# Gating rows' scale and shift applied after the spatial product, and the sample states updated one per two units across the output projection and the u units

## The chip, the cores and the metric

The kernel runs on one core of one Trainium2 chip. The metric is the device time of one execution in microseconds; the profile is of one such execution on the same core. TensorE is called PE, VectorE DVE, ScalarE ACT, GpSimd POOL, and SP is the engine that issues most of the DMAs.

## The reference

The kernel is one inference step of a two-layer hybrid decoder trunk on a prompt of 512 tokens and on 8 sample tokens, all in f32 with a width of 1024. Layer 0 mixes with retention and a chunked gating unit, layer 1 with a convolution module, and each is followed by a squared-ReLU MLP. The part that the change touches is the mixer of layer 0:

```python
z = h @ w_in
q, k, v, g, u, s = jnp.split(z, SPLIT_IDX, axis=-1)
...
o, s_new = retention(q, k, v, s0.astype(jnp.float32))   # S_n = gamma S_{n-1} + k_n^T v_n
...
u = jax.nn.gelu(u, approximate=False)
s = jax.nn.gelu(s, approximate=False).reshape(b, t, SGU_GROUPS, SGU_GD)
s_n = layernorm32(s.astype(jnp.float32), ln_g.reshape(SGU_GROUPS, SGU_GD),
                  ln_b.reshape(SGU_GROUPS, SGU_GD)).astype(h.dtype)
...
mixed = jnp.einsum('gij,bnjgd->bnigd', w_s, s_n.reshape(b, nc, c, SGU_GROUPS, SGU_GD)) \
    + bias[:, :, None]
sgu_out = u * mixed.reshape(b, t, U_W)
y = jnp.concatenate([ret_out, sgu_out], axis=-1) @ w_out
return y, s_new, s_n.reshape(b, t, U_W)
```

`w_s` is a causal 128x128 matrix per group, `ln_g` and `ln_b` are per feature. The new retention states of the 8 samples (8 x 4 heads x 128 x 256) and the normalized rows `s_n` of the 8 sample tokens are outputs.

## The kernel before

**Units.** Activations lie feature by token, as 8 chunks of 128 features by 520 tokens. A projection is done in units: one unit makes 128 output features from a 128x1024 block of weights (512 KB, `load_w`, L122, one DMA on SP into one of four `raw` buffers). To keep f32 precision the weights are split in two halves of four chunks each, into a rounded high part on ACT (L132) and the rest on DVE (L133), `wh` and `wl`, with five buffers for half units. PE then does three products per chunk and half of the tokens (`unit_mm`, L161; `unit_part`, L178, for one half of the tokens): 48 matmuls of 260 columns per unit into a two-bank PSUM tile. There are two such tiles (`mmt`, L103), so a unit starts when the unit before the last has been read out of PSUM by DVE.

**The stages around the change.** After the g and v units come eight s units (`in_units(4096, C)`, L722). Each is read out of PSUM by DVE (L724), put through gelu on ACT and, once per group of two units, handled by `s_tok` (L686): PE transposes the tokens to rows (L697), ACT copies them out, DVE takes mean and variance (L707, L708), does an inverse root in small steps (`rsqrt`, L300) and normalizes in place (L714), and POOL multiplies by the scale rows (L716) and adds the shift rows (L717), 128x1024 per group, and the same for the 8 sample rows (L719, L720). The scale and shift rows are loaded as `ln_row`, broadcast to 128 partitions (L683). In the same stage the retention of the last head is finished (`ret_last`, `ret_gate`) and the samples' retention runs: `ret_sample` (L630) loads each of the 8 states on POOL's queue and multiplies it into `os`, and `ret_sample_out` (L649) normalizes the result and writes the sample columns of `reth` and `retl` (L665, L667).

Then come eight units of the retention half of the output projection, `opr` (L745), of which the first two are done half by half; DVE adds each to `x` (L753), which takes the buffer of a tile that is read last in `ret_sample_out`. Then come the eight u units (L762): DVE reads the unit (L765), ACT does gelu (L766), PE multiplies the normalized rows by the spatial matrix (`mx`, L769), DVE adds the position bias (L772) and multiplies by gelu(u) (L775), and the product is split for the next projection (`sguh` on ACT, L399, and `sgul` on DVE, L400). Last the other half of the output projection, `ops` (L801), with the state sums of the convolution's history (`hist`, L787, L791) beside the end of the u units.

**The sample states' update.** `ret_update(b)` (L635) is written at the end of each u unit. It loads state b again (512 KB, on POOL's queue, into one of three `s0` buffers), loads the sample's v row broadcast to 128 partitions in two parts `vb` (256 KB each, on SP, two `kx` buffers), scales them by k on ACT (L644, four steps), forms gamma x S + k v on DVE (L645, four steps) and stores the state on POOL's queue (L647).

**What sets the order.** Each engine runs its own queue in order. The order is made at build time by a scheduler that takes instructions by priority (as written) when their buffers and inputs would be ready, so work that is written later can move ahead of work that is written earlier. Hand-made exceptions are `tc.high_priority` (used at L736) and `tc.issue_after(ins)`, which queues what a block traces on the engine of `ins` behind `ins`; instructions of the block on other engines stay free. In the kernel before, the scheduler moved five of the eight updates ahead of the first opr unit's add.

Of the kernel before, what the change touches and what calls it, by code (L numbers as in the profile page):

```python
# [76 lines left out]
def trunk_kernel(tc, a, o):  # L77
    nc = tc.nc
    te, ve, se, pe_ = nc.tensor, nc.vector, nc.scalar, nc.gpsimd
    with ExitStack() as st:  # L80
# [34 lines left out]
        def h2(ap):  # L115
            return ap.rearrange("p (h t) -> p h t", h=2)
# [149 lines left out]
        def const(name, shape, ap=None, eng=None):  # L266
            t = cp.tile(shape, F32, name=name)
            if ap is not None:
                (eng or nc.sync).dma_start(t, ap)
            return t  # L270
# [2 lines left out]
            return cp.tile([P, C, TS], F32, name=name, tag="small", bufs=2)  # L273

        x0 = bigt("x0")
        par = const("par", [P, 15, C], a["par"], nc.scalar)
        (G_MIX0, G_FFN0, G_MIX1, G_FFN1, G_FIN, GN_G, B_A, B_G, DW_B, CLN_G, CLN_B, B_OUT, W00, SB0, _S) = range(15)

        def pcol(i, c):
            return par[:, i, c:c + 1]  # L280
# [116 lines left out]

        def split_act(src, hi, lo):
            se.activation(hi, src, AF.Copy)  # L399
            ve.tensor_sub(lo, src, hi.bitcast(F32))  # L400
# [224 lines left out]
        def ret_state(b):  # L625
            S0 = mp.tile([P, NH, DV], F32, name="S0", tag="s0", bufs=3)
            nc.gpsimd.dma_start(S0, a["state_ret"][b].rearrange("h d e -> d h e"))
            return S0

# [2 lines left out]
            for h in range(NH):  # L632
                te.matmul(os_[32 * h:32 * h + TS, :], qm[:, h, b, :], S0[:, h, :], start=False, stop=b == TS - 1)

        def ret_update(b):  # L635
            S0 = ret_state(b)
            vb = []
            for i in range(2):
                t = mp.tile([P, 2 * DV], F32, name="vb", tag="kx", bufs=2)
                nc.sync.dma_start(t, scr[b:b + 1, i * 2 * DV:(i + 1) * 2 * DV].to_broadcast([P, 2 * DV]))  # L640
                vb.append(t)
            for h in range(NH):
                vh = vb[h // 2][:, (h % 2) * DV:(h % 2 + 1) * DV]
                se.activation(vh, vh, AF.Copy, scale=ks[:, h, b:b + 1])  # L644
                ve.scalar_tensor_tensor(out=S0[:, h, :], in0=S0[:, h, :], scalar=float(GAMMA[h]), in1=vh,  # L645
                                        op0=ALU.mult, op1=ALU.add)
# [32 lines left out]
        ln_t = {}  # L679
        for hf in range(2):  # L680
            for i in range(2):
                t = mp.tile([P, 544], F32, name="ln_row", tag="qk", bufs=8)[:, :512]
                nc.sync.dma_start(t, a["sgu_ln"][i:i + 1, hf * 512:(hf + 1) * 512].to_broadcast([P, 512]))  # L683
                ln_t[i, hf] = t

        def s_tok(g):  # L686
            sn = mp.tile([P, NC, DV], F32, name=f"sn{g}", tag="vtm", bufs=NH)
            s_n.append(sn)
            sd = ss_n[:, g * DV:(g + 1) * DV]
            for i in range(3):  # L690
                at_ = aux(f"st{g}_{i}")
                rows = P if i < 2 else TS
                subs = 2 if i < 2 else 1
                for u in range(subs):
                    tok = slice((2 * i + u) * P, (2 * i + u) * P + rows)
                    for j in range(2):
                        te.transpose(at_[:rows, u * DV + j * P:u * DV + (j + 1) * P], gs[2 * g + j][:, tok], ident)  # L697
# [18 lines left out]
            pe_.tensor_tensor(sn, sn, gg.rearrange("p (o e) -> p o e", o=1).to_broadcast([P, NC, DV]), op=ALU.mult)  # L716
            pe_.tensor_tensor(sn, sn, bb.rearrange("p (o e) -> p o e", o=1).to_broadcast([P, NC, DV]), op=ALU.add)  # L717
            dst = ss_n[:, g * DV:(g + 1) * DV]
            pe_.tensor_mul(dst, dst, gg[:TS])  # L719
            pe_.tensor_add(dst, dst, bb[:TS])  # L720

        for c, pt in in_units(4096, C):  # L722
            t = tmp(f"s{c}")
# [18 lines left out]
        x = bigt("x")  # L742
        for c in range(C):
            nc.sync.dma_start(x[:, c, :], a["xT"][:, c, :])
        for c in range(C):  # L745
            pt = mmt(f"opr{c}")
            w = split_w(load_w(a["ab_w_out"], 0, c * P))
            if c < 2:
                for hf in range(2):
                    unit_part(pt[:, hf, :HALF], w, two(reth, retl), slice(hf * HALF, (hf + 1) * HALF))  # L750
            else:
                unit_mm(halves(pt), w, two(reth, retl))
            ve.tensor_tensor(h2(x[:, c, :]), ph2(pt), h2(x[:, c, :]), op=ALU.add)  # L753


        ssT = small("ssT")
# [2 lines left out]
            te.transpose(at_[:, c * TS:(c + 1) * TS], ss_n[:, c * P:(c + 1) * P], ident[:TS, :TS])  # L759
        se.copy(ssT, at_[:, :C * TS].rearrange("p (c t) -> p c t", c=C))  # L760
        sguh, sgul = bigt("sguh", F32R), bigt("sgul", F32R)
        for c, pt in in_units(3072, C):  # L762
            g = c // 2
            t = tmp(f"u{c}")
            ve.tensor_tensor(h2(t), ph2(pt), h2(r0), op=ALU.mult)  # L765
            se.activation(t, t, AF.Gelu)  # L766
            at_ = aux(f"mx{c}")
            for n in range(NC):
                te.matmul(at_[:, n * P:(n + 1) * P], s_n[g][:, n, (c % 2) * P:(c % 2 + 1) * P], wsT[:, g, :],  # L769
                          start=True, stop=True)  # L770
# [4 lines left out]
            ve.tensor_mul(m, m, t)  # L775
# [412 lines left out]
```

## Time and profile before

| what | value |
|---|---|
| median of 3 runs | 1317.03 us (1313.05 to 1317.89) |
| the profiled execution | 1319.12 us, of it the span of the trace 1317.4 us |
| mean granted PE clock | 0.985 |
| busy PE, DVE, ACT, POOL | 1273.5, 923.0, 648.7, 242.7 us |
| DMA | 149.21 MB, mean 113 GB/s |

A window of the trace gives each engine's busy time in a stretch of the span, the clock that PE was granted (1.00 is full speed), and the share of the 16 DMA engines. A timeline row gives start, duration, engine, line, operation, output and inputs, and in square brackets how long the engine had been idle and what released it. A line can be that of a helper: L133 is every split of weights, whatever its stage.

### The profile page before, as it was taken

The page shows a single profiled execution, that of the slowest core. Times are in us where ns is not written, and L with a number is a line of the kernel's source. Part 1 is how long each engine was busy: PE and PEld are TensorE (multiplying, and loading weights), DVE is VectorE, ACT ScalarE, POOL GpSimd, SP SyncE. Part 2 cuts the span into 40 slices and gives each one's busy share as a digit, 9 for nine tenths or more (in the row PEclk, how much of TensorE's full clock was granted, in tenths as well). Part 3 has the DMA queues.
Part 4 walks back from the last instruction along what each step waited for, and adds up shares of the span by engine and source line. Part 5 has one row for each costly group of instructions (what it writes and reads, how often), then busy time and mean ns, then how long its engine had stood idle before and what let it go on. Part 6 is the DMA issues. An engine that isn't in the chain of part 4 may idle for free.

```text
span 1317.4 us, 26073 instructions
## 1 busy us (share of the span) xinstructions
PE 1273.5 (97%) x10618; PEld 1241.4 (94%) x10618; DVE 923.0 (70%) x1634; ACT 648.7 (49%) x1160; POOL 242.7 (18%) x226
## 2 busy tenths in 40 slices
PE   9999999799999999999999999989989999999996
PEld 8999999799998999999999998858989999999995
DVE  6833668965688866766755699968997667676544
ACT  7432343433356643544444476547756445454342
POOL 0521013640020000000000469842200000000012
PEclk9999999899999999999999999999989999999998
DMA  7323235773222323332322322453523333332321
GB/s 281 97 86 104 85 130 193 249 278 111 81 82 81 99 94 97 97 113 81 114 96 96 93 85 81 140 129 112 161 65 97 103 90 101 109 97 81 97 81 65
DMA packets 50407, 149.21 MB, mean 113 GB/s; under 512 B 6112, under 2 KB 13280, under 8 KB 50288
## 3 DMA queue, kind: packets, MB, share of 16 engines
q1 hardware_dynamic: 45888, 134.11, 33.1%
q0 software_dynamic: 3456, 12.58, 2.7%
q8 instruction: 83, 1.36, 0.4%
q10 hardware_dynamic: 944, 0.86, 0.2%
q14 instruction: 36, 0.29, 0.1%
HBM read 139.35 MB, written 9.13 MB: 113 GB/s over the span
## 4 chain that ended last, share of the span: by engine, by line
PE 85%; DVE 9%; issue 2%; ACT 2%; DMA 1%; DVEq 0%; SPq 0%
PE y L161 27%; PE in L161 15%; PE pp L245 12%; PE pq L245 6%; PE ci L161 4%; PE ops L161 3%; PE pr L245 3%; PE f L161 3%; PE opr L161 3%; DVE wl L133 2%; PE co L178 2%; DVE cv L1023 2%; PE cvB L993 1%; PE opr L178 1%; ACT wh L132 0%
## 5 line engine op out<-in xcount | busy, mean ns | idle before, releaser
L132 ACT ACTIVATE wh<-raw 128x512 fp32r<-128x512 f32 x403 | 252.3, 629 | 347.2 <-PE in L161 101.9
L133 DVE TENSOR_TENSOR wl<-raw,wh 128x512 fp32r<-128x512 f32 x403 | 301.0, 749 | 165.8 <-ACT wh L132 159.0
L161 PE MATMUL y<-f,wh 128*128 128x260 f32 x2016 | 323.9, 283 | 0.8 <-DVE x L872 0.8
L161 PEld LDWEIGHTS y<-f,wh 128*128 128x128 f32 x2016 | 275.8, 188 | 1.2 <-DVE x L872 1.2
L161 PE MATMUL y<-f,wl 128*128 128x260 f32 x1008 | 202.6, 282 | 0.0
L161 PEld LDWEIGHTS y<-f,wl 128*128 128x128 f32 x1008 | 155.3, 188 | 0.0
L161 PE MATMUL in<-n0h,wh 128*128 128x260 f32 x640 | 133.0, 287 | 1.2 <-DVE k L470 0.8
L161 PE MATMUL in<-n0l,wh 128*128 128x260 f32 x640 | 130.8, 285 | 1.2 <-DVE n0l L358 1.0
L161 PE MATMUL in<-n0h,wl 128*128 128x260 f32 x640 | 129.6, 284 | 0.1
L132 ACT ACTIVATE wh<-S 128x512 fp32r<-128x512 f32 x116 | 73.1, 631 | 91.4 <-PE y L161 45.5
L133 DVE TENSOR_TENSOR wl<-S,wh 128x512 fp32r<-128x512 f32 x116 | 79.3, 687 | 49.6 <-ACT wh L132 48.4
L161 PEld LDWEIGHTS in<-n0h,wh 128*128 128x128 f32 x640 | 99.0, 188 | 3.6 <-PE in L161 1.3
L161 PEld LDWEIGHTS in<-n0l,wh 128*128 128x128 f32 x640 | 98.7, 188 | 2.7 <-DVE n0l L358 2.5
L245 PE MATMUL pp<-Th,wh 128*128 128x260 f32 x348 | 98.3, 283 | 0.9 <-ACT Th L213 0.9
L161 PEld LDWEIGHTS in<-n0h,wl 128*128 128x128 f32 x640 | 98.6, 188 | 0.4 <-DVE wl L133 0.3
L245 PE MATMUL pp<-Tl,wh 128*128 128x260 f32 x348 | 98.1, 282 | 0.0
L245 PE MATMUL pp<-Th,wl 128*128 128x260 f32 x348 | 97.8, 282 | 0.0
L1016 POOL TENSOR_TENSOR pacc<-pacc,pp 128x512 f32<-128x512 f32 x60 | 88.1, 1478 | 4.5 <-ACT pp L1015 1.7
L374 POOL TENSOR_TENSOR n2acc<-n2acc,n2sq 128x520 f32<-128x520 f32 x5 | 7.0, 1402 | 344.9 <-DVE n2l L358 327.3
L374 POOL TENSOR_TENSOR n4acc<-n4acc,n4sq 128x520 f32<-128x520 f32 x5 | 6.5, 1307 | 346.7 <-ACT n4sq L371 346.7
L245 PEld LDWEIGHTS pp<-Th,wh 128*128 128x128 f32 x348 | 65.5, 189 | 1.4 <-ACT Th L213 1.1
L245 PEld LDWEIGHTS pp<-Tl,wh 128*128 128x128 f32 x348 | 65.5, 188 | 0.0
(406 smaller groups left out, 2919.2 us busy)
## 6 DMA issues: line engine op xcount, KB each, us to landing
raw<-in_ffn_w SPq DMA_DIRECT2D x128, 512.0 KB, 3.6
raw<-in_ab_w_in SPq DMA_DIRECT2D x39, 512.0 KB, 3.7
S<-in_state_ret POOLq DMA_DIRECT2D x16, 512.0 KB, 4.8
raw<-in_ab_w_out SPq DMA_DIRECT2D x16, 512.0 KB, 3.7
raw<-in_conv_w_in SPq DMA_DIRECT2D x16, 512.0 KB, 3.7
raw<-in_conv_w_out SPq DMA_DIRECT2D x16, 512.0 KB, 3.7
X<-xscr SPq DMA_DIRECT2D x32, 132.0 KB, 3.3
x<-in_xT SPq DMA_DIRECT2D x16, 260.0 KB, 5.3
```

Source lines behind the costliest of these rows:

```text
L132: se.activation(hi, sp, AF.Copy)
L133: ve.tensor_sub(lo, sp, hi.bitcast(F32))
L161: te.matmul(pts[hf], wt[:, k % KH, :], x(k, SECOND if hf else FIRST)[i == 1], start=k == order[0] and i == 0, stop=k == order[-1] and i == 2)
L178: te.matmul(pt, wt[:, k % KH, :], xt, start=n == 0 and i == 0, stop=n == C - 1 and i == 2)
L245: te.matmul(bank, wt[:, k, :], xt, start=n in (1, 2, 5) and k == 0 and i == 0, stop=k == KH - 1 and i == 2, skip_group_check=True)
L374: eng.tensor_add(self.acc, self.acc, sq)
L993: te.matmul(acc[32 * g:32 * g + 32, :], diag[c, k][:, g, :], X[:, g, k:k + HC], start=k == 0, stop=k == ns - 1)
L1016: pe_.tensor_add(pacc, pacc, pp)
L1023: ve.scalar_tensor_tensor(out=o, in0=win(k), scalar=dw[:, c, k:k + 1], in1=acc, op0=ALU.mult, op1=ALU.add)
```

## The change

1. The scale and shift of the normalized prompt rows are no longer applied before the spatial product. Since the product runs over positions and scale and shift go by feature, `mixed = scale x (W s) + shift x rowsum(W) + bias`. PE makes the row sums of the masked spatial matrix once, for all groups (`wsum`, a product of 128x512 with a matrix of ones), ACT scales them into `ws`, DVE makes `bias_c = ws x shift + bias` per u unit (128x128), and the mixing sum becomes one step with the scale as a column factor. The two columns come in `par` (16 instead of 15). The 8 sample rows keep scale and shift on POOL, and `ln_row` is loaded for 8 partitions.
2. `ret_update` is cut in two, `ret_load` and `ret_update`. `ret_behind(n, done)` is called after each of the eight opr adds (n = 0 to 7) and after each of the eight u units' splits (n = 8 to 15): an even n loads state n // 2, an odd n updates the state loaded before. Its block is queued behind the add or the split on DVE, which binds the four DVE steps of the update; loads, scalings on ACT and stores are free.
3. The first two opr units are written with their first token halves ahead of their second ones.

```diff
-            se.activation(hi, src, AF.Copy)
-            ve.tensor_sub(lo, src, hi.bitcast(F32))
+            return ve.tensor_sub(lo, src, hi.bitcast(F32))
...
-        def ret_update(b):
-            S0 = ret_state(b)
-            vb = []
+        def ret_load(b):
+            S0, vb = ret_state(b), []
...
+            return b, S0, vb
+
+        def ret_update(b, S0, vb):
...
+        loaded = []
+
+        def ret_behind(n, done):
+
+            with tc.issue_after(done.ins):
+                if n % 2:
+                    ret_update(*loaded.pop())
+                else:
+                    loaded.append(ret_load(n // 2))
...
-            pe_.tensor_tensor(sn, sn, gg.rearrange("p (o e) -> p o e", o=1).to_broadcast([P, NC, DV]), op=ALU.mult)
-            pe_.tensor_tensor(sn, sn, bb.rearrange("p (o e) -> p o e", o=1).to_broadcast([P, NC, DV]), op=ALU.add)
...
+        def opr_add(c, pt):
+            ret_behind(c, ve.tensor_tensor(h2(x[:, c, :]), ph2(pt), h2(x[:, c, :]), op=ALU.add))
+
+        first = [(mmt(f"opr{c}"), split_w(load_w(a["ab_w_out"], 0, c * P))) for c in range(2)]
+        for hf, cols in enumerate((FIRST, SECOND)):
+            for c, (pt, w) in enumerate(first):
+                unit_part(pt[:, hf, :HALF], w, ret, cols)
+                if hf:
+                    opr_add(c, pt)
...
+        at_ = aux("wsum")
+        te.matmul(at_, ones, wsT.rearrange("p g i -> p (g i)"), start=True, stop=True)
+        ws = mp.tile([P, 544], F32, name="ws", tag="qk", bufs=8)[:, :TP].rearrange("p (g i) -> p g i", g=NH)
+        se.activation(ws.rearrange("p g i -> p (g i)"), at_, AF.Copy, scale=float(D))
...
+            ve.scalar_tensor_tensor(out=bias_c, in0=ws[:, g, :], scalar=pcol(SLN_B, c), in1=bias_row[:, g, :],
+                                    op0=ALU.mult, op1=ALU.add)
...
-            ve.tensor_tensor(m[:, :TP].rearrange("p (n t) -> p n t", n=NC), at_.rearrange("p (n t) -> p n t", n=NC),
-                             bias_row[:, g:g + 1, :].to_broadcast([P, NC, P]), op=ALU.add)
+            ve.scalar_tensor_tensor(out=m[:, :TP].rearrange("p (n t) -> p n t", n=NC),
+                                    in0=at_.rearrange("p (n t) -> p n t", n=NC), scalar=pcol(SLN_G, c),
+                                    in1=bias_c.rearrange("p (o t) -> p o t", o=1).to_broadcast([P, NC, P]),
+                                    op0=ALU.mult, op1=ALU.add)
...
-            ret_update(c)
+            ret_behind(C + c, done)
```

**How the order moves.** The first place is DVE's queue at the end of the s units, before the change; `s_2919` is the read of the last s unit (`in_7`) out of PSUM, `olny` and `slny` are the inverse roots of the samples' retention and of the gating rows, and `S_3730` is a sample state.

```order
L133 TENSOR_TENSOR wl<-raw,wh 128x512
L656 TENSOR_SCALAR olnv<-omv 128x1
L645 SCALAR_TENSOR_TENSOR S_3730<-S_3730,vb 128x256 x2
L708 BN_AGGR smv<-sst_2792 8x2
L645 SCALAR_TENSOR_TENSOR S_3730<-S_3730,vb 128x256
L304 TENSOR_SCALAR rs_t<-olnv 128x1
L306 TENSOR_SCALAR rs_vh<-olnv 128x1
L645 SCALAR_TENSOR_TENSOR S_3730<-S_3730,vb 128x256
L711 TENSOR_SCALAR slnv<-smv 128x5
L724 TENSOR_TENSOR s_2919<-in_7_2860,n0r 128x520
```

The same place of the changed kernel, where the read is `s_2913`:

```order
L309 TENSOR_TENSOR rs_t<-rs_t,rs_vh 128x1
L309 TENSOR_TENSOR rs_t<-rs_t,rs_vh 128x5
L310 SCALAR_TENSOR_TENSOR olny<-rs_t,olny 128x1
L310 SCALAR_TENSOR_TENSOR slny<-rs_t,slny 128x5
L734 TENSOR_TENSOR s_2913<-in_7_2854,n0r 128x520
L671 TENSOR_SCALAR ons<-os,omv,olny 128x256
```

No state step stands ahead of the read any more, and the two inverse roots, which stood behind it, now stand ahead of it.

The second place is DVE's queue in the u units. Before, around the second u unit:

```order
L765 TENSOR_TENSOR u_3628<-in_1_3569,n0r 128x520
L772 TENSOR_TENSOR m_3636<-mx_3631,bias_row 128x512
L774 TENSOR_SCALAR m_3636<-ssT,par 128x8
L133 TENSOR_TENSOR wl<-raw,wh 128x512
L775 TENSOR_TENSOR m_3636<-m_3636,u_3628 128x520
L133 TENSOR_TENSOR wl<-raw,wh 128x512
L400 TENSOR_TENSOR sgul<-m_3636,sguh 128x520
L765 TENSOR_TENSOR u_3716<-in_2_3657,n0r 128x520
```

And now:

```order
L788 TENSOR_TENSOR u_3677<-in_1_3618,n0r 128x520
L799 TENSOR_SCALAR m_3687<-ssT,par 128x8
L133 TENSOR_TENSOR wl<-raw,wh 128x512
L795 SCALAR_TENSOR_TENSOR m_3687<-mx_3682,par,bias_c 128x512
L800 TENSOR_TENSOR m_3687<-m_3687,u_3677 128x520
L786 SCALAR_TENSOR_TENSOR bias_c<-ws,par,bias_row 128x128
L400 TENSOR_TENSOR sgul<-m_3687,sguh 128x520
L647 SCALAR_TENSOR_TENSOR S_3612<-S_3612,vb 128x256 x4
L133 TENSOR_TENSOR wl<-raw,wh 128x512
L788 TENSOR_TENSOR u_3761<-in_2_3702,n0r 128x520
```

Four state steps stand between the second unit's `sgul` and the read of the third unit, and one split of weights stands behind them.

The third place is ACT's queue there. Before:

```order
L399 ACTIVATE sguh<-m_3636 128x520
L132 ACTIVATE wh<-raw 128x512
L766 ACTIVATE u_3716<-u_3716 128x520
L132 ACTIVATE wh<-raw 128x512
L399 ACTIVATE sguh<-m_3724 128x520
```

And now:

```order
L399 ACTIVATE sguh<-m_3687 128x520
L132 ACTIVATE wh<-raw 128x512 x2
L646 ACTIVATE vb<-vb,ks 128x256
L789 ACTIVATE u_3761<-u_3761 128x520
L646 ACTIVATE vb<-vb,ks 128x256 x3
L399 ACTIVATE sguh<-m_3771 128x520
```

The first scaling of the next update's v row stands ahead of the third unit's gelu, and the other three ahead of its `sguh`.

More of the change, by code (lines that the diff above doesn't have):

```diff
@@ L275, in trunk_kernel @@
         x0 = bigt("x0")
-        par = const("par", [P, 15, C], a["par"], nc.scalar)
-        (G_MIX0, G_FFN0, G_MIX1, G_FFN1, G_FIN, GN_G, B_A, B_G, DW_B, CLN_G, CLN_B, B_OUT, W00, SB0, _S) = range(15)
+        par = const("par", [P, 16, C], a["par"], nc.scalar)
+        (G_MIX0, G_FFN0, G_MIX1, G_FFN1, G_FIN, GN_G, B_A, B_G, DW_B, CLN_G, CLN_B, B_OUT, W00, SB0, SLN_G, SLN_B) = range(16)
         def pcol(i, c):
@@ L681, in trunk_kernel @@
             for i in range(2):
-                t = mp.tile([P, 544], F32, name="ln_row", tag="qk", bufs=8)[:, :512]
-                nc.sync.dma_start(t, a["sgu_ln"][i:i + 1, hf * 512:(hf + 1) * 512].to_broadcast([P, 512]))
+                t = mp.tile([P, 544], F32, name="ln_row", tag="qk", bufs=8)[:TS, :512]
+                nc.sync.dma_start(t, a["sgu_ln"][i:i + 1, hf * 512:(hf + 1) * 512].to_broadcast([TS, 512]))
                 ln_t[i, hf] = t
@@ L715, in s_tok @@
             gg, bb = [ln_t[i, g // 2][:, (g % 2) * DV:(g % 2 + 1) * DV] for i in range(2)]
-            pe_.tensor_tensor(sn, sn, gg.rearrange("p (o e) -> p o e", o=1).to_broadcast([P, NC, DV]), op=ALU.mult)
-            pe_.tensor_tensor(sn, sn, bb.rearrange("p (o e) -> p o e", o=1).to_broadcast([P, NC, DV]), op=ALU.add)
             dst = ss_n[:, g * DV:(g + 1) * DV]
-            pe_.tensor_mul(dst, dst, gg[:TS])
-            pe_.tensor_add(dst, dst, bb[:TS])
+            pe_.tensor_mul(dst, dst, gg)
+            pe_.tensor_add(dst, dst, bb)
         for c, pt in in_units(4096, C):
@@ L744, in trunk_kernel @@
             nc.sync.dma_start(x[:, c, :], a["xT"][:, c, :])
-        for c in range(C):
-            pt = mmt(f"opr{c}")
[L747 to L753, printed above, removed]
+        ret = two(reth, retl)
+        def opr_add(c, pt):
[6 more added lines that the diff above has]
+                    opr_add(c, pt)
+        for c in range(2, C):
+            pt = mmt(f"opr{c}")
+            unit(pt, a["ab_w_out"], 0, c * P, ret)
+            opr_add(c, pt)
         ssT = small("ssT")
@@ L764, in trunk_kernel @@
             t = tmp(f"u{c}")
+            bias_c = mp.tile([P, TP], F32, name="bias_c", tag="on", bufs=4)[:, :P]
+            ve.scalar_tensor_tensor(out=bias_c, in0=ws[:, g, :], scalar=pcol(SLN_B, c), in1=bias_row[:, g, :],
+                                    op0=ALU.mult, op1=ALU.add)
             ve.tensor_tensor(h2(t), ph2(pt), h2(r0), op=ALU.mult)
@@ L771, in trunk_kernel @@
             m = tmp(f"m{c}")
-            ve.tensor_tensor(m[:, :TP].rearrange("p (n t) -> p n t", n=NC), at_.rearrange("p (n t) -> p n t", n=NC),
-                             bias_row[:, g:g + 1, :].to_broadcast([P, NC, P]), op=ALU.add)
+            ve.scalar_tensor_tensor(out=m[:, :TP].rearrange("p (n t) -> p n t", n=NC),
+                                    in0=at_.rearrange("p (n t) -> p n t", n=NC), scalar=pcol(SLN_G, c),
+                                    in1=bias_c.rearrange("p (o t) -> p o t", o=1).to_broadcast([P, NC, P]),
+                                    op0=ALU.mult, op1=ALU.add)
             ve.tensor_scalar(m[:, TP:], ssT[:, c, :], pcol(W00, c), pcol(SB0, c), op0=ALU.mult, op1=ALU.add)
             ve.tensor_mul(m, m, t)
-            split_act(m, sguh[:, c, :], sgul[:, c, :])
-            ret_update(c)
+            done = split_act(m, sguh[:, c, :], sgul[:, c, :])
+            ret_behind(C + c, done)
         dw = const("dw", [P, C, W], a["dw"])
@@ L1144 @@
         feat(np.repeat(g["sgu_w"][0, :, 0, 0], 256)), feat(np.repeat(g["sgu_b"][0, :, 0], 256)),
-        feat(g["final_norm_g"])], 1)
+        feat(g["sgu_ln_g"][0]), feat(g["sgu_ln_b"][0])], 1)
     taps = np.concatenate([g["conv_dw_w"][0], np.zeros((1, D), np.float32)]).reshape(W + 1, C, 4, 32)
```

## The prediction

> **What bounds the kernel now.** I read the page first, then the stretch that the diff touches in windows, then who waited there, then the timelines of the engines that are waited for.
>
> ```profile
> span 1317.4 us, 26073 instructions
> PE 1273.5 (97%) x10618; PEld 1241.4 (94%) x10618; DVE 923.0 (70%) x1634; ACT 648.7 (49%) x1160; POOL 242.7 (18%) x226
> ```
>
> TensorE (PE) carries the time, so a change elsewhere pays only where PE waits or runs slowly. The windows by stage give seconds of busy time for PE, PEld, DVE, ACT and POOL, then the granted clock, the DMA share and GB/s. They are cut at the ends of the s units, of the output projection's retention half (opr) and of the u units.
>
> ```profile
> 182.00:238.00 56.00, 55.80 (x483) 50.62 (x482) 41.81 (x121) 24.26 (x47) 17.44 (x16) 1.00 0.54 183
> 238.00:267.50 29.50, 21.47 (x139) 20.73 (x138) 26.75 (x85) 10.11 (x23) 21.05 (x26) 0.77 0.81 261
> 267.50:302.50 35.00, 35.00 (x294) 34.84 (x292) 21.67 (x40) 13.05 (x25) 10.54 (x8) 1.00 0.70 248
> 302.50:353.20 50.70, 50.70 (x427) 50.70 (x427) 31.20 (x55) 19.02 (x33) 2.89 (x8) 1.00 0.32 98
> ```
>
> PE is full before 238 and after 267.5. Between them it is idle for 29.50 - 21.47 = 8.03 us and its clock falls to 0.77, while DVE is busy for 26.75 of 29.50. That is the only hole in this part. The waits and PE's timeline (start, duration, engine, what, idle time before it) say where it opens:
>
> ```profile
> PE opr L178 <- DVE olny L305: 5.3, 1, 5.3
> PE opr L178 <- DVE retl L400: 2.3, 1, 2.3
> ...
> 240.99 0.28 PE L178 MATMUL opr<-reth,wl 128*128 128x260 f32 x1
> 246.62 0.59 PE L178 MATMUL opr<-reth,wh 128*128 128x260 f32 x1 [5.34 <-DVE olny L305]
> 247.00 0.42 PE L178 MATMUL opr<-retl,wh 128*128 128x260 f32 x1
> 247.22 0.42 PE L178 MATMUL opr<-reth,wl 128*128 128x260 f32 x1
> 259.21 0.58 PE L178 MATMUL opr<-retl,wh 128*128 128x260 f32 x1 [2.31 <-DVE retl L400]
> ```
>
> After the gap a matmul starts every 0.22 us (247.00 to 247.22); at full clock it is 34.60/288 = 0.120 (a row below). Both gaps end on DVE, so I read DVE beside POOL:
>
> ```profile
> 240.91 2.37 POOL L717 TENSOR_TENSOR sn<-sn,ln_row 128x1024 f32<-128x1024 f32 x1
> 252.66 2.37 POOL L716 TENSOR_TENSOR sn<-sn,ln_row 128x1024 f32<-128x1024 f32 x1
> ...
> 232.44 0.69 DVE L133 TENSOR_TENSOR wl<-raw,wh 128x512 fp32r<-128x512 f32 x1 [3.55 <-PE st L697]
> 236.27 0.68 DVE L724 TENSOR_TENSOR s<-in,n0r 128x520 f32<-128x520 f32 x1
> 236.88 2.27 DVE L133 TENSOR_TENSOR wl<-raw,wh 128x512 fp32r<-128x512 f32 x1
> 241.39 2.44 DVE L133 TENSOR_TENSOR wl<-raw,wh 128x512 fp32r<-128x512 f32 x1
> 245.88 0.68 DVE L724 TENSOR_TENSOR s<-in,n0r 128x520 f32<-128x520 f32 x1
> 253.15 2.17 DVE L645 SCALAR_TENSOR_TENSOR S<-S,vb 128x256 f32<-128x256 f32 x1
> 256.51 2.65 DVE L400 TENSOR_TENSOR retl<-sg,reth 128x64 fp32r<-128x64 f32 x1
> ```
>
> PE's second opr unit needs the PSUM bank of the last s unit. That unit ended at 238.0, but DVE read it (L724) only at 245.88 to 246.56, and PE went on at 246.62. In front of it on DVE stood eight state steps (L645) and two L133 of 2.27 and 2.44 us that take 0.69 elsewhere. Each long row started inside a gating product of POOL and ended some 0.6 us after it: 240.91 + 2.37 = 243.28, and the L133 ended at 243.83. The second gap is the same: L645 behind L716, then L400 of 2.65 us behind L717.
>
> A rule weighed here: the Trainium skill, "SBUF — State Buffer", section "Who interferes with whom", says that a VectorE instruction with two SBUF inputs and a GpSimd instruction that reads SBUF exclude each other, the first one holding the port to its end. The trace agrees: the two-input L133 was held for 2.27 us, and the L724 at 236.27 with one input in PSUM took its plain 0.68.
>
> **The change part by part.**
>
> *The hole.* The work done from 238.00 to 267.57, priced at full clock (from the chain of waits: start, time, what):
>
> ```profile
> 231.17 1.26 PE st L697 x10
> 267.57 34.60 PE opr L161 x288
> 302.18 0.34 PE sst L759 x4
> 325.76 0.89 PE mx L769 x8
> 326.65 5.73 PE in L161 x48
> ```
>
> Two opr units are 96 matmuls, 96 x 0.1201 = 11.53. The ten transposes st are 1.26, four sst 0.34, two ots 2 x 0.11 = 0.22, and the mixing products of three u units, which ran in the hole, 3 x 0.89 = 2.67. Sum 16.02 of 29.57 us: 13.55 us are lost, 8.03 idle and 5.5 by the clock. The products that filled the hole come onto the full path later, which this sum counts already.
>
> *Does the hole close?* By the order, two things leave DVE ahead of that L724: all L645, and the wait for POOL's wide products.
>
> ```profile
> 230.98 0.91 ACT L644 ACTIVATE vb<-vb,ks 128x256 f32<-128x256 f32 x2 [3.63 <-DMA vb<-scr]
> L308 DVE TENSOR_TENSOR rs_t<-slny 128x5 f32<-128x5 f32 x12 | 2.2, 180 | 0.2
> L719 POOL TENSOR_TENSOR ss_n<-ss_n,ln_row 8x256 f32<-8x256 f32 x4 | 4.1, 1026 | 0.0
> ```
>
> From 232.44 to 245.88 DVE needed 13.44 us. Off go eight L645 at 0.38 (3.0) and the stretch of two L133 (2.27 + 2.44 - 2 x 0.69 = 3.3). Some 18 small rsqrt steps move ahead: at most 18 x 0.18 = 3.2, less where two chains overlap; I take 2.2. That leaves 9.3. The start was late too: ACT stood 3.63 us at a broadcast row vb and so held the split of 232.44, for which DVE idled 3.55. So the read comes at 232.44 - 3.55 + 9.3 = 238.2, when the bank has just been filled (238.0), and is over by 238.9, or 239.9 at the upper bound. PE wants it at 241.1. Up to the sample columns' retl then come ons, one split, two rsqrt steps, five normalizing steps and sg: eleven rows with retl, none above the split's 0.69, at most 7.6, so retl stands by 246.5. PE asks for it after the second unit's first half (2.9), st and ots (1.2) and sst, the ones-product and a quarter of a mixing product (1.5), at 246.7. Neither waits. POOL's 8-row steps of 1.0 stay and could hold one two-input row by that much. The work that covers both is these two half units; without it each microsecond that DVE is late costs one.
>
> *Added.* PE gets one ones-product of 128x512, as wide as one unit's mx: 0.89 us, on the path. ACT's copy of it, eight bias_c steps on DVE (0.2 to 0.4 each) and the mixing sum with a column factor instead of L772 lie in DVE's free 19.5 us of the u stage; at most 3.4 us, cost 0. The normalized rows' two large POOL products go: 8 x 2.4 us that nothing waits for any more. The ceiling of the gain is 13.55 - 0.89 = 12.66.
>
> *The state updates moved.* Four go behind opr adds 1, 3, 5, 7, four behind u units 1, 3, 5, 7.
>
> ```profile
> L645 DVE SCALAR_TENSOR_TENSOR S<-S,vb x32: 378/416/3329, 224.9 to 292.9; 128x256 f32<-128x256 f32 x32
> L644 ACT ACTIVATE vb<-vb,ks 128x256 f32<-128x256 f32 x32 | 14.3, 499 | 16.1 <-DMA vb<-scr 16.1
> L766 ACT ACTIVATE u<-u 128x520 f32<-128x520 f32 x8 | 5.1, 640 | 2.4 <-DVE u L765 2.4
> L399 ACT ACTIVATE sguh<-m 128x520 fp32r<-128x520 f32 x8 | 5.1, 632 | 8.5 <-DVE m L775 8.5
> DMA to landing us min/median/max: 3.4/3.9/8.6
> ...
> 339.05 0.70 DVE L765 TENSOR_TENSOR u<-in,n0r 128x520 f32<-128x520 f32 x1 [1.57 <-PE in L161]
> 341.25 0.70 DVE L775 TENSOR_TENSOR m<-m,u 128x520 f32<-128x520 f32 x1
> 342.65 0.70 DVE L400 TENSOR_TENSOR sgul<-m,sguh 128x520 fp32r<-128x520 f32 x1 [0.70 <-ACT sguh L399]
> ```
>
> DVE has room: 31.20 of 50.70 us are used in the u stage, and 16 steps of 0.42 add 6.7. The queue order is what can hurt. The two vb buffers serve one update at a time, so the next vb load waits on SP for the update's last step, and its first scaling stands ahead of the next gelu on ACT. The ring is: vb lands (L, the 3.4/3.9/8.6 row), four scalings and the gelu 2.6, sguh and sgul 1.3, a split 0.7, one unit's chain 339.05 to 343.35 = 4.3, four updates 1.4: L + 10.3, or L + 9.4 if neighbouring rows overlap by 0.08 as these do. A pair of units gives 2 x 6.62 = 13.24. So a landing over 2.9 to 3.9 us makes each of three rounds late by the rest. At the end there is slack:
>
> ```profile
> 359.38 0.69 DVE L400 TENSOR_TENSOR sgul<-m,sguh 128x520 fp32r<-128x520 f32 x1
> 361.36 0.40 PE L161 MATMUL ops<-sgul,wh 128*128 128x260 f32 x2
> ```
>
> The last sgul was ready at 360.07 and PE used it at 361.36: 1.3 us. With L = 3.9 the loss is 3 x (3.9 - 2.9) - 1.3 = 1.7 or 0; I take 1.2, towards the upper end, since the state's store starts beside the vb load. SP's weight loads queue behind vb too, but the five half-unit split buffers keep splits some 1.5 units (1.5 x 6.62 = 10 us) ahead: 0.
>
> *Sum.* 12.66 - 1.2 = 11.5 us. The profiled execution took 1319.12 us for its span of 1317.4, so it would take 1307.6. The median of the runs shown, 1317.03, lies 2.1 below it; 11.5 off the median gives 1305.5.
>
> **The rivals.**
>
> *Part of the hole stays.* If the long DVE rows are not POOL's doing, or another step is late, DVE is 3.3 us later at the bank, 1.2 past PE, and 3.4 later again at retl. A stall of 3 us also costs clock: from 259.21, after 2.31 us idle, some 26 matmuls ran 0.10 slower, 2.5 us. Gain 12.66 - 3 - 2.5 = 7.2, or 1309.8. The overlaps above speak against it. The Trainium skill, "TensorE: Matmul & The Clock Gate", section "Part 1: The HAM clock gate (the "warmup" mystery)", lowers the clock after an idle window of about 3.4 us; by that the stall would cost 3 alone and the gain be 9.7. The 2.31 us row disagrees, so I keep 7.2. Chance 0.13.
>
> *The ring costs more.* With L of 5 to 6, between the median and the longest, the loss is 2.0 to 5.0 at the mild bound: gain 7.7 to 10.7, or down to 5 at the harsh one; about 1309. The u stage's DMA share of 0.32 speaks against, the store and the load of 512 KB that come into it for. Chance 0.13.
>
> *Nothing gained, or slower.* The same ring with L = 8.6, the longest landing, each time: 3 x (8.6 - 3.9) - 1.3 = 12.8, the whole gain; 1317.2. Chance 0.05. From L = 10.8 it loses over 19.3 and the kernel is slower by more than 0.5%; at L = 11 it is 20.0 lost, 12.66 won: 1324.4. The place is DVE's row of four updates ahead of the split and of the next unit's PSUM read. Chance 0.03; no landing shown is that long.
>
> **How the numbers follow.** The forecast, gain 10 to 12.7, has 0.66. The range adds the two partial cases and the spread of single runs (1313.05 to 1317.89): 1301.5 to 1311.5. About 0.5%, 6.6 us, is what a measurement of this kernel can tell from no change. Faster by more: 0.66 plus most of the two partial cases, 0.87; within: 0.09; slower: 0.04.
>
> **What would show it.** Right: from the end of the s units to the end of the u units 102.5 to 104 us instead of 115.2, PE's clock 1.00 throughout, no DVE L133 over 1.5 us there, the last s unit's bank read within 1 us of its end, and PE's only wait at ops' first unit, under 2 us. Wrong: waits of the second opr unit on DVE as now, or u-unit matmuls waiting for DVE while ACT waits for vb.

## The result and the profile after

The changed kernel takes 1306.82 us (median of 4 runs, 1305.69 to 1307.07) against 1316.07 us for the kernel before beside it (4 runs, 1313.05 to 1317.89): a ratio of 0.9923, with a 95% interval of 0.9907 to 0.9939. Its profiled execution has a span of 1304.9 us against 1317.4. The page's first rows:

```profile
span 1304.9 us, 26074 instructions
PE 1267.9 (97%) x10620; PEld 1234.7 (95%) x10620; DVE 911.6 (70%) x1642; ACT 648.7 (50%) x1161; POOL 224.4 (17%) x218
```

The windows answer to those of before (us of busy time of PE, PEld, DVE, ACT and POOL, then PE's granted clock, DMA share, GB/s). They are cut at the end of the s units, where the third opr unit begins, at the end of opr and at the end of the u units:

```profile
182.00:237.86 55.86, 55.33 (x481) 50.20 (x480) 40.11 (x149) 22.58 (x42) 10.53 (x15) 1.00 0.51 161
237.86:253.60 15.74, 15.74 (x123) 14.60 (x122) 13.06 (x49) 5.78 (x11) 2.33 (x4) 1.00 0.60 197
253.60:288.40 34.80, 34.80 (x292) 34.66 (x290) 16.17 (x31) 11.94 (x25) 7.88 (x8) 1.00 0.72 228
288.40:341.00 52.60, 52.60 (x445) 52.58 (x445) 38.48 (x73) 25.22 (x48) 12.63 (x22) 1.00 0.63 200
```

PE is busy for 15.74 of 15.74 us where it was busy for 21.47 of 29.50, and the clock stays at 1.00. The hole is gone, and none has opened in the u stage. A sharper measure than the span is used from here on, the **stretch**: from the start of the first opr matmul to the start of the first ops matmul in PE's timeline.

```profile
238.00 0.37 PE L178 MATMUL opr<-reth,wh 128*128 128x260 f32 x1
...
341.02 0.48 PE L161 MATMUL ops<-sguh,wh 128*128 128x260 f32 x2
```

Here it is 103.02 us. In the kernel before the same two starts are 238.14 and 352.93, 114.79 us. The stretch is 11.77 shorter, the span 12.5.

The DVE timeline shows the read of the last s unit's bank (L734, before L724) and the sample columns' `retl`:

```profile
238.06 0.70 DVE L734 TENSOR_TENSOR s<-in,n0r 128x520 f32<-128x520 f32 x1 [0.43 <-PE in L161]
...
243.60 0.21 DVE L400 TENSOR_TENSOR retl<-sg,reth 128x64 fp32r<-128x64 f32 x1
...
L133 DVE TENSOR_TENSOR wl<-raw,wh 128x512 fp32r<-128x512 f32 x32 | 21.9, 692 | 12.7 <-ACT wh L132 12.6
```

The read begins at 238.06, and DVE itself waited 0.43 us for PE there: it has time to spare. `retl` is ready at 243.81. The last row groups the weight splits of 238 to 341 us: 32 of them, 692 ns each, none held.

### The profile page after: what moved, and what is told of

The parts are those of the page before. It is cut to its first block, busy times and chain, and to the rows that moved or that the text cites. A ratio compares the mean times of both kernels' runs of the same rounds, so it can differ in the third digit from the quotient of the medians.

```text
span 1304.9 us, 26074 instructions
## 1 busy us (share of the span) xinstructions
PE 1267.9 (97%) x10620; PEld 1234.7 (95%) x10620; DVE 911.6 (70%) x1642; ACT 648.7 (50%) x1161; POOL 224.4 (17%) x218
## 4 chain that ended last, share of the span: by engine, by line
PE 86%; DVE 8%; ACT 2%; issue 2%; DMA 1%; DVEq 0%; SPq 0%
PE y L161 28%; PE in L161 16%; PE pp L245 13%; PE pq L245 6%; PE ci L161 4%; PE pr L245 3%; PE opr L161 3%; PE ops L161 3%; PE f L161 2%; DVE wl L133 2%; PE co L178 2%; DVE cv L1048 2%; PE cvB L1018 1%; PE opr L178 1%; PE mx L792 1%
## 5 line engine op out<-in xcount | busy, mean ns | idle before, releaser
L133 DVE TENSOR_TENSOR wl<-raw,wh 128x512 fp32r<-128x512 f32 x403 | 294.1, 733 | 164.8 <-ACT wh L132 161.5
L133 DVE TENSOR_TENSOR wl<-S,wh 128x512 fp32r<-128x512 f32 x116 | 79.3, 687 | 49.0 <-ACT wh L132 47.8
```

The costliest lines, as they stand in the source:

```text
L133: ve.tensor_sub(lo, sp, hi.bitcast(F32))
```

## Experiments

All kernels were run beside the kernel before, five rounds each; its medians there were 1316.92 to 1317.28. Three explanations of the old hole were set against each other. **A**, the prediction's: the eight state steps on DVE and the DVE rows held by POOL's wide products together. **B**: the state updates alone. **C**: POOL's products alone. "Rest" is the span after the stretch's end; times are in us. The scheduler makes a new order for each kernel, so a difference of a microsecond or two between two of them can be the order's.

| run | what | stretch | span | rest | median | ratio to before (95%) |
|---|---|---|---|---|---|---|
| before | | 114.79 | 1317.4 | 964.5 | 1316.07 | |
| after | | 103.02 | 1304.9 | 963.9 | 1306.82 | 0.9923 (0.9907-0.9939) |
| e1 | gating only | 119.86 | 1321.7 | 964.4 | 1321.81 | 1.0041 (1.0025-1.0057) |
| e2 | after, old gating | 101.91 | 1304.5 | 964.5 | 1306.68 | 0.9920 (0.9906-0.9934) |
| e3 | after, unread POOL products | 102.76 | 1303.3 | 962.9 | 1305.62 | 0.9913 (0.9898-0.9928) |
| e4 | before again | 114.66 | 1316.7 | 964.7 | 1317.63 | 0.9999 (0.9988-1.0011) |
| e5 | updates moved only | 101.90 | 1305.9 | 966.0 | 1306.61 | 0.9922 (0.9908-0.9936) |
| e6 | before, four vb buffers | 117.61 | 1320.2 | 964.6 | 1318.80 | 1.0019 (1.0010-1.0028) |
| e7 | before, one vb pair | 112.20 | 1312.3 | 962.6 | 1313.55 | 0.9974 (0.9965-0.9983) |
| e8 | after, vb loaded twice | 110.48 | 1319.4 | 970.7 | 1318.97 | 1.0017 (1.0006-1.0028) |
| e9 | gating only, one vb pair | 111.49 | 1311.7 | 962.5 | 1315.05 | 0.9993 (0.9983-1.0004) |
| e10 | e8 with four vb buffers | 106.21 | 1314.4 | 970.3 | 1314.40 | 0.9983 (0.9971-0.9994) |
| e11 | after, five ones-products | 106.50 | 1308.2 | 962.5 | 1309.57 | 0.9949 (0.9934-0.9964) |
| e12 | after again | 103.02 | 1302.2 | 961.2 | 1306.81 | 0.9923 (0.9908-0.9937) |

**e1, the gating change alone.** The kernel before with these edits; the updates and the first opr units stay as they were:

```diff
-            pe_.tensor_tensor(sn, sn, gg.rearrange("p (o e) -> p o e", o=1).to_broadcast([P, NC, DV]), op=ALU.mult)
-            pe_.tensor_tensor(sn, sn, bb.rearrange("p (o e) -> p o e", o=1).to_broadcast([P, NC, DV]), op=ALU.add)
+        te.matmul(at_, ones, wsT.rearrange("p g i -> p (g i)"), start=True, stop=True)
...
+            ve.scalar_tensor_tensor(out=bias_c, in0=ws[:, g, :], scalar=pcol(SLN_B, c), in1=bias_row[:, g, :],
...
```

> The kernel before with the gating change alone (no wide POOL products, the ones-product added); state updates and the first units as before. Theory A (both the eight state steps on DVE and the DVE rows held by POOL made the hole): the rows of 2.27 and 2.44 us fall to 0.7, so the last s unit's bank is read 3.3 us earlier, at about 242.6 instead of 245.9, PE's wait there falls from 5.3 to about 2 us, and the wait at retl goes. With some slow clock behind the wait the gain is 13.55 - 0.89 - 2 - 2.5 = about 8 us, 5 to 10.5: ratio to the kernel before 0.992 to 0.996. Theory B (the state steps alone; the held rows were hidden): gain under 3 us, ratio above 0.998. Theory C (POOL's products alone): nearly all of it, over 11.5 us, and no PE wait between the s and the u units.

It is slower than before, by 0.41% (0.25 to 0.57). The two held splits did vanish, but the read did not come early. DVE's timeline, ACT's at the same time, and PE's waits:

```profile
240.05 0.43 DVE L647 SCALAR_TENSOR_TENSOR S<-S,vb 128x256 f32<-128x256 f32 x1 [2.65 <-ACT vb L646]
242.15 0.82 DVE L647 SCALAR_TENSOR_TENSOR S<-S,vb 128x256 f32<-128x256 f32 x2 [1.09 <-ACT vb L646]
243.07 0.69 DVE L133 TENSOR_TENSOR wl<-raw,wh 128x512 fp32r<-128x512 f32 x1
243.87 0.69 DVE L734 TENSOR_TENSOR s<-in,n0r 128x520 f32<-128x520 f32 x1
```

```profile
239.51 0.91 ACT L646 ACTIVATE vb<-vb,ks 128x256 f32<-128x256 f32 x2 [4.21 <-DMA vb<-scr]
241.61 0.91 ACT L646 ACTIVATE vb<-vb,ks 128x256 f32<-128x256 f32 x2 [1.19 <-DMA vb<-scr]
```

```profile
PE opr L161 <- DVE x L758: 6.2, 1, 6.2
PE opr L178 <- DVE s L734: 4.1, 1, 4.1
```

The split takes 0.69 and not 2.44, yet DVE stands 2.65 and 1.09 us in front of it, because its state steps wait for ACT, and ACT waits 4.21 and 1.19 us for vb rows on their way. The read comes at 243.87. Later the same pair of waits holds the opr adds, and PE waits 6.2 us there. A and C fall: the time that the held rows gave back went into other waits. B stands.

**e2, the old gating put back into the changed kernel.** The reverse of e1's edit; updates and first units as changed.

> The changed kernel with the old gating: POOL's two wide products per group are back, the ones-product and the bias columns are out; state updates and the first units stay as changed. Theory A: two or three DVE rows of over 2 us come back between the s units and the u units, the last s unit's bank is read some 3 us later, PE waits there 1 to 2 us and again 1 to 3 us at retl, and the clock falls behind it: about 4 to 8 us of the gain are lost, the 0.89 us of the ones-product won back; span 1308 to 1312. Theory B: span 1304 (0.9 under the changed kernel), no PE wait. Theory C: span 1316.

As B said: PE without a wait, and the stretch 1.11 us shorter than in the changed kernel, which is about the ones-product that is out. POOL's products hold DVE rows again, and longer than in the kernel before (DVE, then POOL):

```profile
228.19 2.88 DVE L133 TENSOR_TENSOR wl<-raw,wh 128x512 fp32r<-128x512 f32 x1
245.69 1.57 DVE L723 TENSOR_SCALAR slnv<-smv 128x5 f32<-128x5 f32 x1
254.41 6.43 DVE L647 SCALAR_TENSOR_TENSOR S<-S,vb 128x256 f32<-128x256 f32 x4
...
244.88 2.35 POOL L729 TENSOR_TENSOR sn<-sn,ln_row 128x1024 f32<-128x1024 f32 x1
252.50 3.65 POOL L728 TENSOR_TENSOR sn<-sn,ln_row 128x1024 f32<-128x1024 f32 x1 [4.57 <-DVE sn L726]
```

Four state steps take 6.43 us against 1.41 in the changed kernel, and PE waits for none of what stands behind them on DVE (splits and opr adds).

**e3, POOL products that nobody reads.** The changed kernel with two extra POOL products per group, written to a scratch tile:

```diff
...
+            for _ in range(2):
+                pe_.tensor_tensor(scrap, sn, sn, op=ALU.mult)
```

> The changed kernel with two extra POOL products of 128x1024 per group that read sn twice and write a scratch tile nobody reads: POOL is as busy as in the kernel before, but no instruction waits for the product itself (POOL's own 8-row steps queue behind it). Theory A with the SBUF port as the cause: two-input DVE rows that start inside such a product last 2 us and more, as in the kernel before, and the span grows to 1307 to 1312, about as with the old gating. If what cost time in the kernel before was the wait for the product's result, no row is held, and the span stays at 1305.

Both halves of the question have an answer. Rows are held by a product whose result no one waits for (four state steps 4.90 us, a split 2.38), so the holding is one of access and not of data. Here the trace agrees with the Trainium skill, "SBUF — State Buffer", "Who interferes with whom", by which a VectorE instruction with two SBUF inputs and a GpSimd instruction that reads SBUF exclude each other. And the stretch stays at 102.76: the holding costs nothing here.

**e4, the kernel before again.** No edit.

> The kernel before, unchanged, as a second profile and a control: ratio 1.000. The profiled execution shown lies 2 us above the timed median. If the executions of the kernel before differ by how long the hole lasts, this profile's stretch from the end of the s units to the end of the u units differs from 115.2 us by as much as its span differs from 1317.4, and every other stretch agrees within 0.5 us.

The stretch agrees within 0.13 us (114.66 and 114.79): the hole was the same in both. The spans differ by 0.7, and that lies ahead of the stretch, which starts 0.76 earlier here. Two profiles so close to one another do not show what makes the kernel's times spread from 1313 to 1320; the last section has such a pair for the changed kernel.

**e5, the updates moved alone.** The kernel before with `ret_load`, `ret_update` and `ret_behind` as in the change, the old gating and the old loop of the first two opr units.

> The kernel before with the state updates moved alone: a vb load and a state step behind every opr add and u unit, as in the changed kernel; old gating, and the first two opr units written as before. After the runs above Theory B stands (the updates among the s units alone made the hole). It expects what the kernel with the old gating and the new first units gave: span 1304 to 1306, ratio 0.991 to 0.993, and no PE wait between the s and the u units. If the order of the first units' halves is a part of the cause, PE waits at the second opr unit or at retl by 2 us or more: span 1309 to 1313.

The whole gain, with the stretch of e2 to 0.01 us. Neither the gating nor the order of the first halves has a part in it. PE in windows cut as above:

```profile
238.00:254.00 16.00, 16.00 (x133) 15.49 (x131) 14.67 (x46) 5.18 (x10) 7.67 (x6) 1.00 0.58 196
...
288.40:340.00 51.60, 51.60 (x438) 51.60 (x436) 36.81 (x69) 24.75 (x49) 13.55 (x23) 1.00 0.63 213
```

**e6, four vb buffers in the kernel before.**

```diff
-                t = mp.tile([P, 2 * DV], F32, name="vb", tag="kx", bufs=2)
+                t = mp.tile([P, 2 * DV], F32, name="vb", tag=("kx", "kz")[b % 2], bufs=2)
```

> The kernel before with four vb buffers in place of two (the updates take the two tiles kx and the two tiles kz in turn, no other edit). Theory B1 (ScalarE, which works in order, stands at vb scalings whose row has not landed, since an update's load waits for the update before, and holds the splits and gelus behind it): loads run one update ahead, ScalarE's waits for vb between 225 and 262 us (some 13 us) fall under 5, and 6 us or more of the hole go: ratio 0.991 to 0.995. Theory B2 (the state steps on DVE themselves, 0.38 us each with what they wait for, are what stands ahead of the last s unit's read): the hole stays within 3 us, ratio 0.998 to 1.002.

Inconclusive for B1: the edit did not take away what it was to take away. ACT waits 16.9 us for vb between 210 and 265, against 10.4 in the kernel before. The rows now land 3.1, 5.2 and 9.4 us after issue (least, median, most) against 3.4, 3.9 and 8.6, and the order made for it brings 24 state steps ahead of the first opr add where there were 20. It is slower by 0.19% (0.10 to 0.28).

**e7, one vb pair in the kernel before.** All eight updates use one row pair, loaded and scaled once; seven loads and their scalings are left out.

```diff
-            vb = []
-            for i in range(2):
...
+            if not once:
+                for i in range(2):
...
-                vh = vb[h // 2][:, (h % 2) * DV:(h % 2 + 1) * DV]
-                se.activation(vh, vh, AF.Copy, scale=ks[:, h, b:b + 1])
+                vh = once[h // 2][:, (h % 2) * DV:(h % 2 + 1) * DV]
```

> The kernel before with one vb row pair, loaded and scaled once, used by all eight state updates: the other seven loads and their scalings are left out (the state then takes the first sample's row in every step), while the 32 state steps, the state's loads and its stores stay. Theory B1: no vb wait on ScalarE is left, so most of the hole goes: ratio 0.990 to 0.994. Theory B2: the DVE steps still stand ahead of the read, the hole stays within 3 us: ratio 0.997 to 1.001. The state's own load (3 to 8 us from issue to landing) could hold DVE in place of vb; then DVE shows waits for S.

No wait of ACT for vb is left, and the stretch is 2.59 us shorter: inside what B2 expected (within 3 us, ratio 0.997 to 1.001). DVE has hardly a gap any more (busy for 25.52 of the 27.50 us from 237.5), and rows held by POOL carry the delay:

```profile
232.52 3.53 DVE L133 TENSOR_TENSOR wl<-raw,wh 128x512 fp32r<-128x512 f32 x1
237.94 4.25 DVE L647 SCALAR_TENSOR_TENSOR S<-S,vb 128x256 f32<-128x256 f32 x4
243.06 1.41 DVE L647 SCALAR_TENSOR_TENSOR S<-S,vb 128x256 f32<-128x256 f32 x4
244.52 0.68 DVE L726 TENSOR_TENSOR s<-in,n0r 128x520 f32<-128x520 f32 x1
```

So it looks as if each of the two holds stood in for the other, which asks for the run without both.

**e9, neither held rows nor vb waits.** e1's kernel with e7's edit; the same seven loads and scalings are left out.

> The kernel before with the new gating (as in the gate-only kernel) and one vb row pair loaded and scaled once and used by all eight updates (seven loads and their scalings left out; the state takes the first sample's row in every step). Two things that hold DVE are then gone together: rows held by POOL's wide products, and splits and steps that wait on ScalarE for a vb row. Taking away either alone left the last s unit's bank read at 243.9 and 244.5 us. If they cover one another (Theory E, either of them is enough to hold the read back), removing both closes the hole although all 32 state steps stay in it: no PE wait over 1 us, span 1303 to 1308, ratio 0.990 to 0.994. If the state steps on DVE are what counts (B2), the read stays 3 us or more behind the end of the s units: PE waits 2 to 4 us, span 1309 to 1314.

The read comes 3.2 us earlier than in e1, at 240.70, and PE waits only 0.5 us for it. But theory E falls all the same: PE now waits in small pieces on the sample columns' chain behind it (`ons` and `ots` are their normalized rows and the transposes), and is granted a clock of 0.86 there. The window of the hole, PE's waits, then DVE's for the state itself:

```profile
237.70:262.00 24.30, 18.71 (x126) 17.10 (x125) 22.44 (x99) 4.74 (x9) 11.57 (x18) 0.86 0.78 269
...
PE ots L677 <- DVE ons L674: 2.1, 1, 2.1
PE mx L794 <- DVE sg L680: 1.4, 1, 1.4
PE opr L178 <- DVE retl L400: 0.8, 1, 0.8
...
PE opr L178 <- DVE s L737: 0.5, 1, 0.5
...
DVE S L650 <- DMA S<-in_state_ret: 3.2, 3, 1.4
```

The stretch is 111.49, 8.5 us above the changed kernel with the same gating, and the span lies in B2's range (1309 to 1314). By the medians nothing is won over the kernel before (0.9983 to 1.0004); the profiled execution was the fastest of its twelve. The order differs too: twelve state steps stand between the split and the read, where the kernel before had eight. How the 8.5 us divide between the steps' own time, the wait for states and their transfers was not separated.

**e8, every vb row loaded twice in the changed kernel.** It prices the ring, the chain in which an update's load waits for the update before:

```diff
                 nc.sync.dma_start(t, scr[b:b + 1, i * 2 * DV:(i + 1) * 2 * DV].to_broadcast([P, 2 * DV]))
+                nc.sync.dma_start(t, scr[b:b + 1, i * 2 * DV:(i + 1) * 2 * DV].to_broadcast([P, 2 * DV]))
```

> The changed kernel with every vb row loaded twice into the same tile, one after the other, so that its landing takes 8 us and not 4. The ring of the prediction: in the opr stage a round then takes about 15 us against 11.5 for its two units, in the u stage 13.6 + 4 = 17.7 against 13.24; three rounds each are late by 3.5 and 4.4 us, together 23, of which the split buffers and the slack at the output projection's first unit take some 6. So 10 to 20 us lost, span 1315 to 1325, with PE waits for DVE at opr and at u units or at the first ops unit. If the ring does not matter (the rival that its price was never there), the span stays within 2 us of 1305.

The ring is real: 14.5 us of span, 12.2 us of the median, and the kernel is slower than before by 0.17% (0.06 to 0.28). The stretch takes 7.5 of the span's loss. The other 6.8 follow in the first ops unit, where PE waits 3.0 us for the last `sguh` and runs twice for some 3 us at about half its clock (0.53 from 350 to 352 and from 362 to 364). Update by update, the first scaling on ACT, then PE's waits:

```profile
304.80 0.51 ACT L647 ACTIVATE vb<-vb,ks 128x256 f32<-128x256 f32 x1 [8.46 <-DMA vb<-scr]
322.75 0.91 ACT L647 ACTIVATE vb<-vb,ks 128x256 f32<-128x256 f32 x2 [2.60 <-DMA vb<-scr]
340.94 0.91 ACT L647 ACTIVATE vb<-vb,ks 128x256 f32<-128x256 f32 x2 [4.75 <-DMA vb<-scr]
```

```profile
PE in L161 <- DVE u L789: 4.2, 3, 2.7
PE ops L161 <- ACT sguh L399: 3.0, 1, 3.0
PE ops L161 <- DVE u L789: 2.3, 1, 2.3
```

Counted from these scalings the rounds are 17.95 and 18.19 us, where 17.7 was expected; counted from the state steps on DVE (313.08, 329.12, 345.88) they are 16.04 and 16.76. In the opr stage PE does not wait at all, against the expectation. The stock of splits made ahead is the likely cover; no run varied it.

**e10, the same with four vb buffers** (e6's edit on e8's kernel).

> The kernel of the doubled vb loads, with four vb buffers in place of two. Ring theory: an update's loads no longer wait for the update before, so the doubled landing runs beside it; the loss of 12 to 14 us goes, span 1304 to 1309. If the loss was the second loads' traffic on the queue, and not the ring, it stays above 1314.

In between: 4.3 us of stretch come back, 3.2 remain, and the rest stays at 970.3, so that the span of 1314.4 just meets the mark of the traffic theory. Neither theory alone gives this. Counted through the trace, the loads do run one update ahead: the rows issued at 309.64, behind the steps of 308.66, are used by the steps of 341.36 and not by those of 325.33. But their scaling moved ahead too. ACT takes it at 318.97 after waiting 3.22 us for the rows (at 336.41 after 3.99), with splits and a gelu of the u units behind it in its queue. So with four buffers the landing still holds ACT, and PE still waits 3.1 us for the last `sguh`.

**e11, the ones-product five times.**

```diff
-        te.matmul(at_, ones, wsT.rearrange("p g i -> p (g i)"), start=True, stop=True)
+        for _ in range(5):
+            te.matmul(at_, ones, wsT.rearrange("p g i -> p (g i)"), start=True, stop=True)
```

> The changed kernel with the ones-product of 128x512 issued five times in place of once. TensorE is full from the s units to the end of the u units, so each extra product costs what it lasts, 0.85 to 0.96 us: 3.4 to 3.9 us longer, span 1308.5, ratio to the kernel before 0.9945 to 0.996. If such a product is hidden, the span stays at 1305.

The stretch grows by 3.48 us, 0.87 per product: it is on the path, and the prediction's 0.89 was its price. The medians differ by 2.8.

**e12, the changed kernel again.** No edit.

> The changed kernel, unchanged, on the same chip as the others of this call: ratio 0.992, span 1304 to 1306, as the reference for differences of a microsecond.

The stretch is 103.02 again, to the hundredth; the span, 1302.2, lies below the 1304 to 1306 expected (last section). e5 and e2 are 1.1 us shorter in it, but their medians (1306.61, 1306.68) are not told from 1306.81, so no version here beats the changed kernel by a measurable amount.

## Why the prediction was right, and where its reasons failed

**The hole: right.** It was priced at 13.55 us lost. e5 removes it, adds nothing to PE, and has PE full and at 1.00 throughout; its stretch is 12.89 shorter, so that much was lost. The price of the work at full clock, 16.02 us, was some 0.7 too low; no run shows in which item.

**The times at which DVE gets there: right.** The read was forecast for 238.2 and begins at 238.06, where DVE had already waited 0.43 us for the bank; `retl` was forecast by 246.5 and is ready at 243.81. Of PE's waits none is left; one under 2 us at the first ops unit was allowed for.

**The causes: wrong in their shares.** The step that failed is "Off go eight L645 at 0.38 (3.0) and the stretch of two L133 (2.27 + 2.44 - 2 x 0.69 = 3.3)". It treats DVE's 13.44 us as a sum in which each item comes off. e1 took the 3.3 off and the read of the bank, counted from the first opr matmul, came at 243.87 - 237.40 = 6.5 us instead of 245.88 - 238.14 = 7.7; e7 took the vb waits off and it came at 244.52 - 237.52 = 7.0. Against kernels whose PE is full throughout (101.90 without the ones-product, 103.02 with it) the stretch loses 12.9 us in the kernel before, 16.8 without the held rows, 10.3 without the vb waits and 8.5 without either. The updates reach DVE by three ways, the port, ACT's wait for vb, and the state's own load with the steps, and it looks as if each covers a part of the others; how they divide is open. What has to leave is the updates, and that part of the change did all of it (e5). The overlap of held rows and POOL products, which the prediction gave as evidence, is real (e3). That it cost time was only argued: taken out alone it won nothing (e1), put back it costs nothing (e2, e3), and only with the vb waits gone as well is less lost without it, 8.5 us against 10.3.

**The gating change: it costs about a microsecond of the stretch and returns nothing that was measured.** "Added ... 0.89 us, on the path" is right (0.87 by e11). What it was to buy, rows not held, is covered once the updates are gone (e2, e5).

**The vb ring: the mechanism right, the loss mis-sized.** 1.2 us were taken, between 0 and 1.7; it cost nothing that PE shows. The changed kernel's u stage, first DVE (state steps, the reads of units five and seven counted from zero, the last `sgul`), then ACT's scalings:

```profile
304.89 1.83 DVE L647 SCALAR_TENSOR_TENSOR S<-S,vb 128x256 f32<-128x256 f32 x4
318.16 1.43 DVE L647 SCALAR_TENSOR_TENSOR S<-S,vb 128x256 f32<-128x256 f32 x4
327.15 0.70 DVE L788 TENSOR_TENSOR u<-in,n0r 128x520 f32<-128x520 f32 x1 [0.27 <-PE in L161]
331.43 1.42 DVE L647 SCALAR_TENSOR_TENSOR S<-S,vb 128x256 f32<-128x256 f32 x4
340.68 0.69 DVE L788 TENSOR_TENSOR u<-in,n0r 128x520 f32<-128x520 f32 x1
347.82 0.69 DVE L400 TENSOR_TENSOR sgul<-m,sguh 128x520 fp32r<-128x520 f32 x1
```

```profile
322.78 0.51 ACT L646 ACTIVATE vb<-vb,ks 128x256 f32<-128x256 f32 x1 [1.82 <-DVE m L795]
336.44 0.51 ACT L646 ACTIVATE vb<-vb,ks 128x256 f32<-128x256 f32 x1 [2.21 <-DMA vb<-scr]
...
DMA to landing us min/median/max: 3.4/4.1/5.2
```

The state steps come every 13.27 us, the pace of the units themselves (13.24), and at 327.15 DVE still waits 0.27 us for PE: the ring just closes in time. Its loads go out on SP at 305.67, 318.94 and 332.21, 0.78 us after the first of four steps, since the first vb buffer is free after two of them; the prediction's upper bound had "four updates 1.4" there. From a load to its first scaling pass 3.84 us in the second round (318.94 to 322.78), and the rest of the ring is 13.27 - 0.27 - 3.84 = 9.2, near the lower bound of 9.4. Only the third round, with 4.23 us, is late: its read, at 340.68, finds the unit waiting. The last `sgul` ends 7.49 us after the first ops matmul (348.51 - 341.02), in the kernel before 7.14 (360.07 - 352.93): 0.35 later, inside the slack of 1.3. The rivals with a dearer ring did not come about, but e8 shows that they were real: with the landing about doubled the change would have lost everything that it won, as the rival at 1317.2 had it.

**The sum.** 11.5 us were forecast, out of a ceiling 0.9 too high and a ring loss 1.2 too high; the stretch gave 11.77. The two errors cancel. The medians differ by 9.25 us, and the ratio's interval makes it 8.0 to 12.2.

## What to carry to other kernels

When several holds lie one behind the other on an engine that works in order, their times do not come off one by one: taking one away shows the next, and only an experiment for each tells what it is worth. Here it paid to move the whole side task out of the crowded stretch, and nothing was won by making a neighbour in that stretch cheaper. An overlap of two slow rows can show that one holds the other, not that anyone waits for it: look for what stands behind it and how large its stock is.

## What the runs showed of the hardware

**A longer wait can leave the clock alone, and a shorter one halve it.** In e8, 2.69 us of idle PE left the clock at full speed, and 2.27 us some 16 us later halved it. In PE's timeline, with two matmuls per row, the rows that follow are 0.24 us apart in the first case (333.19, 333.43) and 0.43 in the second (349.24, 349.67):

```profile
332.88 0.48 PE L161 MATMUL in<-n0h,wh 128*128 128x260 f32 x2 [2.69 <-DVE u L789]
333.19 0.40 PE L161 MATMUL in<-n0l,wh 128*128 128x260 f32 x2
...
348.67 0.77 PE L161 MATMUL ops<-sguh,wh 128*128 128x260 f32 x2 [2.27 <-DVE u L789]
349.24 0.64 PE L161 MATMUL ops<-sgul,wh 128*128 128x260 f32 x2
```

The Trainium skill, "TensorE: Matmul & The Clock Gate", "Part 1: The HAM clock gate (the "warmup" mystery)", has a window of about 3.4 us that runs freely, whatever the kernel does. That the outcome hangs on more than the length of the wait agrees with this; that the gate falls only after an idle window of 3.4 us does not, with 2.27 us here and 2.31 in the kernel before.

**The clock also spreads the times.** The two profiles of the changed kernel have the same stretch, and spans of 1304.9 and 1302.2. In the hundred us in which they differ most, PE is equally busy and the granted clock differs. The window and the group of matmuls that makes most of the difference (after, then e12):

```profile
841.00:941.00 100.00, 92.82 (x994) 76.46 (x994) 77.41 (x134) 63.92 (x123) 35.26 (x35) 0.97 0.47 133
856.52 6.11 PE L1018 MATMUL cvA<-X,diag 128*32 128x256 f32 x64 [4.85 <-DMA X<-xscr]
```

```profile
841.00:941.00 100.00, 92.86 (x1013) 78.48 (x1012) 80.02 (x139) 66.13 (x128) 33.95 (x35) 1.00 0.49 138
856.38 3.69 PE L1018 MATMUL cvA<-X,diag 128*32 128x256 f32 x64 [3.68 <-POOL pacc L1041]
```

The same 64 matmuls take 6.11 us behind a wait of 4.85 and 3.69 behind one of 3.68. PE's waits around them add up to about the same (0.75 and 4.85, 1.79 and 3.68). Whether the length of the single wait or its moment decided was not separated.

**A row with one input was held too.** L723 in e2, a TENSOR_SCALAR with one SBUF input of 128x5, took 1.57 us and ended with a POOL product (247.26 and 247.23); in the changed kernel it took 0.17. The Trainium skill, "SBUF — State Buffer", "Who interferes with whom", names such an operation as able to use both ports in a fast mode and then to contend with GpSimd. The trace agrees for this one row.
